# Keeping split MLP weights in DRAM after the first of four token groups

## The chip, the cores and the metric

One core of a Trainium2 chip runs one launch of the kernel. The metric is device time in microseconds (us). TensorE multiplies matrices, VectorE (DVE), ScalarE (ACT) and GpSimd (POOL) work elementwise, and SyncE (SP) issues nearly all DMA transfers between DRAM and the on-chip SBUF. TensorE writes its products to PSUM banks. Each engine, SP's queue of DMA issues included, takes its instructions in a fixed order and waits at a semaphore where an input is not there or a buffer is not free.

## What is computed

The reference is one layer of a streaming encoder over 2064 tokens (16 meta tokens and 2048 frames) of width 1024: RMSNorm, an input projection, an RWKV-7 recurrence for eight heads, forgetting attention for eight heads, then the part that the change touches:

```
h = h + concatenate([y_rw, y_fx]) @ w_o            # 1024 x 1024
h = h + conv_ffn(rmsnorm(h, norm2_g), ...)         # per token group
# conv_ffn: p = x @ w_in (1024 x 5632); causal depthwise convolution of width 3;
#           u, g = split(p); out = (silu(g) * u) @ w_out (2816 x 1024)
```

All data are float32. The kernel multiplies in a float32r type with fewer bits: each operand is split into a rounded high part and the rest as a low part, and a product is made of high x high, high x low and low x high.

## The kernel before

**Stages.** `phase1` makes the projections and the recurrence. `tail` (L1202) then runs attention beside the output projection and the MLP. The MLP works in four groups of some 512 tokens (`FGROUPS`, L1054), each in two blocks of about 256 tokens. Per group `w_o` (L1083) adds the output projection and normalises, and `mlp` (L1188) goes over 22 pieces of 128 channels, two at a time: `up` (L1145) of two pieces, then `down` (L1173) of the two pieces before them. One pass through that loop uses six weight blocks of 128 x 1024: two for each `up`, two for the `down`. A group has eleven such passes. The first group runs beside attention, the second partly; the third and fourth run alone.

**Weights.** Every group loads all weights anew: `weight` (L1070) calls `split_weight` (L74), which issues one DMA of 512 KB on SP into `ww_raw` (L78), lets ACT round it into `ww_hi` (L81) and DVE subtract to get `ww_lo` (L82). The rings are (3, 2) at L1206: three buffers for `ww_hi`, three for `ww_lo`, two for `ww_raw`. A ring's buffer is written again once TensorE has done its last product with it. The first group's `w_o` is cut in two halves of the input channels (`PARTS`), so its blocks are 128 x 512 and there are sixteen.

**Products.** `product` (L1077) issues, for one PSUM bank, first all products with the high weights and high inputs, then high weights with low inputs, then low weights with high inputs. In `up` a bank takes 24 matmuls with one weight block; with two token blocks and two weight blocks that is 96 per call. In `down` a bank takes six matmuls with the two blocks of the pair, and all sixteen banks' worth of them use both blocks.

**Order of the work.** The order on each engine is not that of the program text. The builder (L1292, `schedule_with_timeline_sim=True`) orders the instructions ahead of time by its own estimate of when each could start, earlier program text first among those that are ready, and then fixes one queue per engine. On the chip nothing is reordered.

**DRAM scratch.** `trunk` (L1256) takes scratch tensors from a DRAM pool for operands that pass between stages.

Of the kernel before, what the change touches and what calls it, by code (L numbers as in the profile page):

```python
# [26 lines left out]
# columns of the packed per-feature parameters  # L27
# [8 lines left out]
# columns of the constant input  # L36
# [4 lines left out]
# rings of tiles of RWKV's columns, by tags  # L41
# [3 lines left out]
FXPOS = (10, 11)                           # groups of the recurrence that come before the attention's operands  # L45
class Pool:
    """A tile pool whose tiles get numbered names."""
# [15 lines left out]
def pools(*args):  # L63
    """a function that takes tiles from one of several pools, by their tags; the last one for the others"""
    *ps, where = args
    return lambda shape, tag, bufs=1, dt=F32: ps[where.get(tag, -1)](shape, tag, bufs, dt)
# [7 lines left out]
def split_weight(K, sp, src, shape, tag, bufs, raw_bufs=1):  # L74
    """DMA a weight block and split it into two float32r parts (hi + lo)."""
    nc = K.nc
    raw = sp(shape, tag + "_raw", bufs=raw_bufs)
    nc.sync.dma_start(raw, src)  # L78
    hi = sp(shape, tag + "_hi", bufs=bufs, dt=F32R)
    lo = sp(shape, tag + "_lo", bufs=bufs, dt=F32R)  # L80
    nc.scalar.copy(hi, raw)  # L81
    nc.vector.tensor_sub(lo, raw, hi.bitcast(F32))  # L82
    return hi, lo


def split(eng, K, src, hi, lo):
    """src as a sum of two float32r parts"""
    K.nc.scalar.copy(hi, src)
    eng.tensor_sub(lo, src, hi.bitcast(F32))


def spread(K, pool, r, n, out, root=True):
    """r [tokens, n tiles of g groups] -> r^-1/2 (or r as it is), repeated over the features of its group, [features, tokens]."""
# [12 lines left out]
def phase1(K, ctx, outer, mixer, between):  # L106
    """RMSNorm, input projection, RWKV and attention operands (all [feature, token])."""
    nc, tc = K.nc, K.tc
    # tiles that are needed longer lie higher, for the MLP to take their place early
# [8 lines left out]
    K.idle = sp                            # tiles that the part after the recurrence's operands leaves free  # L118

    # derived parameter columns: 1-mu, w0/2, a0/2, k_a/2, 1-k_a/2, -q_g/8  # L120
# [20 lines left out]
    TT = tp([128, 4, 17, 64], "TT")        # (I - A_ab)^-T of each head and chunk of the half  # L141
# [3 lines left out]
    ahead = None                           # scaled tiles of the next half's first block  # L145

    def norm_scale(t0, n, tags):
        """tiles of 128 tokens of [t0, t0+n), scaled by 1/rms and by g1"""
        o = PC["g1"][0]
        for s in range(0, n, 128):  # L150
# [3 lines left out]
            # the place of the inverses is free  # L154
# [9 lines left out]
            if t0 == 0:  # L164
                # at the start the columns of the last block are free
# [21 lines left out]
    def norm_split(slot, tiles):  # L187
        """hi/lo [128, 8, n] float32r of the scaled tiles"""
# [30 lines left out]
    def head_sums(out, x, hi, lo):  # L219
        """sums of x over the features of a head, on each of them"""  # L220
# [4 lines left out]
    def rw_part(rp, half, blocks, xb):  # L225
        """RWKV columns: token shift, low-rank parts, decays; the operands of the recurrence go to DRAM."""
# [5 lines left out]
        def tmp(ring):  # L232
            """the next tile of a ring, some of them from tags of the attention's part"""
# [5 lines left out]
        def shift(p, M, n, np_, m, out):  # L239
            """token shift: out = (1-mu) h[t] + mu h[t-1]; pads of the last chunk are zero."""  # L240
# [11 lines left out]
        # the last 32 of the gate's inputs three times: [hi; hi; lo] of the weights, [hi; lo; hi] of the inputs  # L252
        gup2 = rp([128, 1088], "k2b", 2, F32R)[0:96, 0:512]
        thad = rp([128, 1088], "thad")
        # --- low-rank inputs: wd|ad, gd (160) and the forget logits
# [56 lines left out]
        # --- RWKV pairs of heads  # L312
        def k_part(p_):
# [5 lines left out]
            for b, (t0, n) in enumerate(blocks):  # L319
# [6 lines left out]
                # normalised kk  # L326
# [14 lines left out]
                # decay  # L341
# [11 lines left out]
                # in-context learning rate: ta = tanh((a0 + ad a_up)/2), a = (1+ta)/2  # L353
# [20 lines left out]
                # A_ab^T (rows s, columns t > s): first head on partitions 64-127, second on 0-63  # L374
# [62 lines left out]
    def invert(rp, parts, nc_, n):  # L437
        """T^T = (I - A_ab)^-T in place in TT: diagonal blocks of n by forward substitution, one system per
        partition (SY[s][t] = A^T, X[j][t] = T^T); then T21 = T2 A21 T1 on the tensor engine."""
# [35 lines left out]
    def merge(rp, pp, T1):  # L475
        """T21 = T2 A21 T1 of the 64x64 inverses (its transpose into TT)"""
# [19 lines left out]
    def gate_part(blocks, xb):  # L496
        """output gate of the attention heads; block by block, so that the normalised columns are free early"""
# [13 lines left out]
    def fx_part(blocks, xb):  # L511
        """attention heads: q, k normalised per head, v transposed"""
# [57 lines left out]
def forget_cumsum(K, sp, sm):  # L570
    """c = cumsum(log_sigmoid(fl + b_f)) along the tokens, for the 8 heads."""
# [11 lines left out]
    nc.vector.tensor_tensor(s, e, d, op=ALU.mult)          # s = e/(2+e); log1p(e) = 2 atanh(s)  # L583
# [7 lines left out]
    # running sums of each piece, then the totals of the pieces before it  # L591
# [15 lines left out]
def layout(inp):  # L607
    """Host side: only lays the inputs out (transposes, reshapes, concatenations, constants of the shapes)."""
# [34 lines left out]
    mu[1824:1856] = mu[1856:1888] = mu[1792:1824]      # as the columns of wg2  # L643
# [16 lines left out]
    # RWKV mask for [k~;b~] rows s against [a~|r~] columns t: s < t for a~, s <= t for r~  # L660
    s, t = i % 64, i % 64
    cst[:, CM : CM + 128] = np.where(i[None] < 64, s[:, None] < t[None], s[:, None] <= t[None])
    # causal mask of a diagonal attention block, added to c: 0 where key <= query
    cst[:, CIN : CIN + 128] = np.where(i[None] <= i[:, None], 0.0, 1e30)
    # pieces before a piece, of the same head
# [23 lines left out]
PA, PB, PCH = 2, 1, 1                      # banks of the products, the solutions and the chain  # L689


def rwkv(K, ctx, part):
    """RWKV-7 recurrence in chunks of 64 tokens; a group is 2 chunks (at the end 1) of all 4 pairs of heads.

    The first head of a pair (h0) has its k~ rows on partitions 0-63 and its b~ rows on 64-127, the
    second (h1) the other way round, so that their small products use different parts of the array.
    What does not depend on the state is worked out ahead of the chain over the chunks, in two steps that
    overlap with it.
    """
    nc, tc = K.nc, K.tc  # L700
    side = "right" if part else None
    # what the last group norm needs lies above, for the attention to take the place of the others early
# [7 lines left out]
    kr = HS                                # rows of k~ and V of each head  # L710
    br = HS[::-1]                          # rows of b~, A~ and U of each head

    # h0 I v a~ r~, h1 r~ a~ v I; the identities stay
# [5 lines left out]
    def products(G):  # L719
        """the products of a group among k~, b~, a~ and r~, and its transposes; slots are chunk-major"""  # L720
# [3 lines left out]
        kb = K.idle([128, KC, 128], ("T1", "sq0")[odd]).rearrange("p a (j e) -> p a j e", e=64)[:, :n]     # h0 k~ b~, h1 b~ k~  # L724
# [4 lines left out]
        # KG: h0 [k~;b~ natural | A_r^T], h1 [A_r^T | b~;k~ natural];  AA: A_ak^T  # L729
        G.KG = KG = sp([128, NS, 2, 128], "KG", 2)  # L730
        AA = sp([128, NS, 64], "AA", 2)
        for c in range(0, n, 4):
            for h in range(2):
                gp = ps([128, 4, 128], "pa", PA)
                rhs = xv[HS[h], :, 2 - 2 * h : 4 - 2 * h]        # h0 a~ r~, h1 r~ a~
# [5 lines left out]
        # natural layouts: KG gets k~, b~; VU: V; AN slot 0: A~  # L741
# [17 lines left out]
    def solve(G):  # L759
        """U0 = T A_ak V, the update of the state M' and R' with T applied to A~"""  # L760
        ch0, ncl, xv, KG, VU, AA, AN = G.ch0, G.ncl, G.xv, G.KG, G.VU, G.AA, G.AN
        n = 4 * ncl
        # AN slot 1: A_ak V
# [5 lines left out]
        # [T A~ | U0] = T [A~ | A_ak V]  # L769
# [9 lines left out]
        # MT: h0 [I + M' | r~ + R'], h1 [r~ + R' | I + M']  # L779
# [8 lines left out]
    def chain(G):  # L788
        """the chain over the chunks; the state's rows 0-63 are h0, 64-127 h1, block diagonal"""
        ch0, ncl, KG, VU, MT = G.ch0, G.ncl, G.KG, G.VU, G.MT  # L790
        end = ("pb", PB) if ch0 == NCH - 1 else ("ch", PCH)   # the other products are done
        Y = sp([128, 4, 2, 64], "Y", 2)                      # rows: tokens of the two chunks; pair; heads
# [23 lines left out]
    def norm(G):  # L816
        """the group norm and the gate"""
# [6 lines left out]
        # group norm over the 64 channels of a head  # L824
# [31 lines left out]
def attention(K, ctx, name, phases, bufs, banks):  # L856
    """Forgetting attention: a function that adds a phase, of phases: lists of blocks of query tiles of 128 (-1: the
    meta tokens); in each phase one head after the other. mask: the causal mask is added on the tensor engine."""
# [16 lines left out]
    def load_head(h, qa, nk_all):  # L875
# [3 lines left out]
        kq = sp([128, NK + NR], "kq", nhead, F32R)           # k_hi twice, q_hi and q_lo  # L879
# [29 lines left out]
    def pieces(qa, nk):  # L909
        """ranges of tokens to load: keys only, then keys and queries"""  # L910
# [7 lines left out]
    def softmaxes(hd, qt):  # L918
        """softmax of the query tiles of a block; their tiles share one where they fit"""
# [6 lines left out]
    def softmax(hd, i, P):  # L926
        """P = exp(S - max) of query tile i (-1: the meta tokens), [queries, keys], and 1/sum (from -S, as q comes negated)."""
# [44 lines left out]
    def value(hd, qt, soft):  # L972
        """O^T of the query tiles qt: sum over the key tiles of [v_hi | v_lo]^T P^T."""
# [5 lines left out]
        per = 2 if N <= 256 else 1             # key tiles at a time  # L979
# [34 lines left out]
        # 1/sum along the columns of O^T  # L1014
# [20 lines left out]
    # the scores of a block come before the values of the one before  # L1035
# [25 lines left out]
class Ffn:  # L1061
    """Output projection, residual, RMSNorm and the gated convolutional MLP, in four groups of tokens."""

    def __init__(self, K, W, rings):
        self.K, self.W, self.rings = K, W, rings
        nc = K.nc
# [189 lines left out]
def trunk(tc, args, out, shapes):  # L1256
    K = SimpleNamespace(nc=tc.nc, tc=tc, outT=out, **args)
    with ExitStack() as c0:
        dr = Pool(tc, c0, "scratch", DRAM)
        for name, shape in SCRATCH.items():  # L1260
            setattr(K, name, dr(list(shape), "d_" + name))
# [35 lines left out]
```

## Time and profile before

| | |
|---|---|
| time, median of 3 runs | 3463.82 us (3456.46 to 3465.52) |
| span of the profiled execution, first to last instruction | 3459.8 us |
| what lies around that span | not recorded; the span lies within the range of the runs |
| matmuls | 28651 |
| DMA moved | 377.32 MB |

The span is cut into stretches in some views. Busy time of an engine is the time in which it had an instruction under way; PE is TensorE's matmuls, PEld its loads of weights into the array. A matmul's record overlaps that of the next, so the pace of TensorE is read from the distance of starts, not from the duration of one. "What ended the idle time" names the instruction whose semaphore came last before an engine went on.

### The profile page before, as it was taken

What the parts mean: (1) busy time and instruction counts of PE and PEld (TensorE: products, weight loads), DVE (VectorE), ACT (ScalarE), POOL (GpSimd) and SP (SyncE); (2) the same over time, 40 slices, a digit from 0 to 9 for tenths busy, and PEclk for the clock granted to TensorE, in tenths of its full rate; (3) what the DMA queues carried; (4) which work ended last, traced back from release to release, by engine and by line L of the source; (5) the groups of instructions that cost most, each with busy time, mean ns of one, the idle gap of its engine ahead of it and who ended that gap; (6) DMA issues with size and microseconds to landing.
All of it is one profiled execution on the core that took longest, in us unless ns stands there. A gap on an engine that the chain in (4) does not pass through costs nothing.

```text
span 3459.8 us, 73945 instructions
## 1 busy us (share of the span) xinstructions
PE 3373.8 (98%) x28651; PEld 3219.1 (93%) x28651; DVE 2361.0 (68%) x5338; ACT 1762.1 (51%) x4230; POOL 994.2 (29%) x1270
## 2 busy tenths in 40 slices
PE   7999999999999999999999999999999999999999
PEld 7889889988988987999999999999999999999999
DVE  5655576575566757877788777877765667656666
ACT  5543444554344467765666666664444444444443
POOL 4441113344111257533233345312114111131111
PEclk9999999999999999999999999999999999999999
DMA  3455343255534264333323352324224222232222
GB/s 113 119 127 161 95 109 95 96 124 141 147 96 104 81 181 141 105 105 109 93 83 94 98 160 87 94 71 137 95 94 154 92 92 96 94 108 94 93 92 92
DMA packets 354088, 377.32 MB, mean 109 GB/s; under 512 B 169240, under 2 KB 284168, under 8 KB 352712
## 3 DMA queue, kind: packets, MB, share of 16 engines
q1 hardware_dynamic: 353544, 372.52, 36.2%
q8 instruction: 226, 3.70, 0.4%
q14 instruction: 126, 1.03, 0.1%
q0 software_dynamic: 192, 0.07, 0.0%
HBM read 302.22 MB, written 70.27 MB: 108 GB/s over the span
## 4 chain that ended last, share of the span: by engine, by line
PE 80%; DMA 7%; DVE 5%; issue 3%; POOL 2%; ACT 2%; SPq 1%; POOLq 0%; ACTq 0%; DVEq 0%
PE pp L1081 32%; PE pr L1081 12%; PE pj L203 5%; PE pj L205 5%; PE pj L204 5%; PE o L1008 4%; PE pt L995 3%; DMA raw<-d_qk 2%; PE pa L737 2%; DMA xv<-d_var 2%; PE s L946 1%; PE s L948 1%; PE pb L774 1%; PE ch L802 1%; PE pb L785 1%
## 5 line engine op out<-in xcount | busy, mean ns | idle before, releaser
L1081 PE MATMUL pp<-xh,ww_hi 128*128 128x256 f32 (+1 forms) x3072 | 467.6, 284 | 11.6 <-ACT zh L1169 3.5
L1081 PE MATMUL pp<-xl,ww_hi 128*128 128x256 f32 (+1 forms) x3072 | 466.1, 285 | 2.3 <-POOL xl L1143 1.8
L81 ACT CAST ww_hi<-ww_raw 128x1024 fp32r<-128x1024 f32 (+1 forms) x304 | 307.9, 1026 | 314.7 <-PE pr L1081 193.1
L1081 PE MATMUL pp<-xh,ww_lo 128*128 128x256 f32 (+1 forms) x3072 | 456.5, 284 | 0.0
L1170 POOL TENSOR_TENSOR zl<-cv,zh 128x256 fp32r<-128x256 f32 (+1 forms) x176 | 174.0, 989 | 940.8 <-ACT pp L1156 430.7
L82 DVE TENSOR_TENSOR ww_lo<-ww_raw,ww_hi 128x1024 fp32r<-128x1024 f32 (+1 forms) x304 | 370.8, 1230 | 87.0 <-ACT ww_hi L81 77.1
L1081 PEld LDWEIGHTS pp<-xh,ww_hi 128*128 128x128 f32 x3072 | 410.1, 189 | 16.8 <-ACT zh L1169 3.6
L1081 PEld LDWEIGHTS pp<-xl,ww_hi 128*128 128x128 f32 x3072 | 410.4, 190 | 5.9 <-POOL xl L1143 3.5
L1081 PEld LDWEIGHTS pp<-xh,ww_lo 128*128 128x128 f32 x3072 | 405.3, 189 | 1.6
L1004 DVE TENSOR_TENSOR pl<-pt,ph 128x512 fp32r<-128x512 f32 (+4 forms) x416 | 220.6, 538 | 80.0 <-ACT ph L1003 77.0
L1003 ACT CAST ph<-pt 128x512 fp32r<-128x512 f32 (+4 forms) x416 | 190.5, 467 | 161.4 <-PE pt L995 112.9
L1183 DVE TENSOR_TENSOR acc<-acc,pr 128x256 f32<-128x256 f32 x480 | 197.8, 420 | 100.8 <-PE pr L1081 99.3
L1160 DVE SCALAR_TENSOR_TENSOR cv<-pp,pc,cv 128x256 f32<-128x256 f32 (+1 forms) x352 | 168.5, 479 | 137.4 <-ACT cv L1159 134.6
L939 DVE CUSTOM_DVE_ANT_0 P<-cb,s 16x16 f32<-16x16 f32 (+8 forms) x360 | 183.0, 519 | 50.6 <-PE s L948 27.1
L995 PE MATMUL pt<-cst,P 128*128 128x128 f32 (+2 forms) x1224 | 201.7, 276 | 3.6 <-ACT P L965 2.0
L1159 ACT ACTIVATE cv<-pp,pc 128x256 f32<-128x256 f32 (+1 forms) x352 | 201.2, 571 | 0.0
L1008 PE MATMUL o<-ph,vs 128*128 128x256 f32 (+3 forms) x640 | 189.4, 303 | 6.8 <-ACT ph L1003 5.1
L1081 PE MATMUL pr<-zh,ww_hi 128*128 128x256 f32 x960 | 193.9, 282 | 0.1
L1081 PE MATMUL pr<-zh,ww_lo 128*128 128x256 f32 x960 | 192.5, 281 | 0.0
L1081 PE MATMUL pr<-zl,ww_hi 128*128 128x256 f32 x960 | 191.4, 280 | 0.0
L1008 PE MATMUL o<-pl,vs 128*128 128x256 f32 (+3 forms) x640 | 174.8, 290 | 2.2 <-DVE pl L1004 1.8
L1161 DVE SCALAR_TENSOR_TENSOR cv<-pp,pc,cv 128x256 f32<-128x256 f32 (+1 forms) x352 | 169.1, 480 | 6.6
(383 smaller groups left out, 8570.4 us busy)
## 6 DMA issues: line engine op xcount, KB each, us to landing
ww_raw<-in_fin_dram SPq DMA_DIRECT2D x176, 512.0 KB, 3.2
ww_raw<-in_fout_dram SPq DMA_DIRECT2D x88, 512.0 KB, 3.9
w_raw<-in_wt_dram SPq DMA_DIRECT2D x60, 512.0 KB, 3.5
xv<-d_var SPq DMA_DIRECT2D x32, 384.0 KB, 5.9
ww_raw<-in_wo_dram SPq DMA_DIRECT2D x24, 512.0 KB, 3.3
raw<-d_qk SPq DMA_DIRECT2D x112, 88.0 KB, 2.6
cb<-d_cd SPq DMA_DIRECT2D x8, 1032.0 KB, 6.8
out_dram<-acc SPq DMA_DIRECT2D x32, 256.0 KB, 2.8
```

The source lines that it names most:

```text
L81: nc.scalar.copy(hi, raw)
L82: nc.vector.tensor_sub(lo, raw, hi.bitcast(F32))
L203: nc.tensor.matmul(p, wh[:, c, :M], xh[:, c, :n], start=c == 0, stop=False)
L939: nc.vector.tensor_tensor_reduce(dst, c, src, 1.0, 3e38, op0=ALU.add, op1=ALU.min, accum_out=mx[:nq, np_ : np_ + 1])
L995: nc.tensor.transpose(pt[:kn, x, c0 : c0 + nq], P[:nq, k0 : k0 + kn], K.ident[:nq, :nq])
L1003: nc.scalar.copy(ph[:kn, xs, c:N], pt[:kn, xs, c:N])
L1004: nc.vector.tensor_sub(pl[:kn, xs, c:N], pt[:kn, xs, c:N], ph[:kn, xs, c:N].bitcast(F32))
L1008: nc.tensor.matmul(o[:, c:N], vs[:kn, jj], pp[:kn, x, c:N], start=jj == 0 and y == 0, stop=jj == nt - 1 and y == 1)
L1081: self.K.nc.tensor.matmul(p, w, x, start=i == 0, stop=i == len(mms) - 1)
L1159: nc.scalar.activation(v, p[:, 2 : nb + 2], AF.Identity, bias=pcol(K, "cb", i), scale=pcol(K, "cw2", i))
L1170: nc.gpsimd.tensor_sub(zl[:, b : b + nb], u, zh[:, b : b + nb].bitcast(F32))
L1183: nc.vector.tensor_tensor(a, a, p, op=ALU.add)
```

## The change

The first use of a weight block goes as before, and afterwards SP issues two more DMAs, which write the two parts to DRAM tensors. A later use of the same block allots the next buffers of the `ww_hi` and `ww_lo` rings and fills each by a DMA of 512 KB from there; no `ww_raw`, no ACT and no DVE instruction is used. Comment lines removed by the diff are left out here; the rings stay (3, 2).

```diff
         self.K, self.W, self.rings = K, W, rings
         nc = K.nc
+        self.done = set()
+        self.split = {name: [K.dram([n, 128, KC * 128], f"{name}_{t}") for t in "hl"]
+                      for name, n in (("wo", KC), ("fin", 2 * FT), ("fout", FT))}
...
-    def weight(self, src, n=KC * 128):
-        return split_weight(self.K, self.W, src, [128, n], "ww", *self.rings)
+    def weight(self, name, i, cc=range(KC)):
+
+        K, nc = self.K, self.K.nc
+        n = 128 * len(cc)
+        cut = lambda t: t[i].rearrange("p c f -> p (c f)")[:, 128 * cc[0] : 128 * cc[0] + n]
+        src = K.__dict__[name]
+        src = cut(src) if name != "fout" else src[i]
+        kept = [self.split[name][x][i, :, 128 * cc[0] : 128 * cc[0] + n] for x in range(2)]
+        if (name, i, cc[0]) in self.done:
+            both = []
+            for t, k in zip(("hi", "lo"), kept):
+                w = self.W([128, n], "ww_" + t, self.rings[0], F32R)
+                nc.sync.dma_start(w.bitcast(F32), k)
+                both.append(w)
+            return both
+        self.done.add((name, i, cc[0]))
+        both = split_weight(K, self.W, src, [128, n], "ww", *self.rings)
+        for w, k in zip(both, kept):
+            nc.sync.dma_start(k, w.bitcast(F32))
+        return both
...
-                wh, wl = self.weight(K.wo[m, :, cc[0] : cc[-1] + 1].rearrange("p c f -> p (c f)"), 128 * len(cc))
+                wh, wl = self.weight("wo", m, cc)
...
-        w = [self.weight(K.fin[i].rearrange("p c f -> p (c f)")) for i in (f, FT + f)]
+        w = [self.weight("fin", i) for i in (f, FT + f)]
...
-        w = [self.weight(K.fout[f]) for f in fs]
+        w = [self.weight("fout", f) for f in fs]
...
         dr = Pool(tc, c0, "scratch", DRAM)
+        K.dram = dr
```

## Rows read from the trace of the kernel before

**Rows 1.** Engines over the span: busy us (share) xinstructions.

```profile
PE 3373.8 (98%) x28651; PEld 3219.1 (93%) x28651; DVE 2361.0 (68%) x5338; ACT 1762.1 (51%) x4230; POOL 994.2 (29%) x1270
```

**Rows 2.** Stretches of the tail: length, busy us of each engine, clock, DMA share, GB/s.

```profile
core 0: us, PE busy (x) PEld busy (x) DVE busy (x) ACT busy (x) POOL busy (x), PEclk, DMA share, GB/s
...
1400.00:1990.00 590.00, 584.34 (x4589) 565.05 (x4588) 469.86 (x1321) 379.10 (x909) 200.66 (x314) 1.00 0.32 99
1990.00:2400.00 410.00, 403.92 (x3211) 391.76 (x3210) 310.98 (x814) 253.03 (x570) 142.33 (x213) 1.00 0.35 111
...
2460.00:3460.00 1000.00, 988.23 (x8276) 985.35 (x8274) 666.16 (x1284) 428.66 (x1057) 176.51 (x174) 1.00 0.29 100
```

**Rows 3.** Chain that ended last, in order of time: start us, us, instructions.

```profile
3232.50 7.11 PE pr L1081 x60
3239.61 21.87 PE pp L1081 x184
...
3266.66 7.11 PE pr L1081 x60
```

**Rows 4.** Waits of PE from 1990 to 3460: us, times, longest us.

```profile
PE pp L1081 <- ACT zh L1169: 3.5, 1, 3.5
PE pp L1081 <- ACT ww_hi L81: 2.3, 2, 1.1
```

**Rows 5.** Costliest groups of the page: the split of the weights.

```profile
L81 ACT CAST ww_hi<-ww_raw 128x1024 fp32r<-128x1024 f32 (+1 forms) x304 | 307.9, 1026 | 314.7 <-PE pr L1081 193.1
...
L82 DVE TENSOR_TENSOR ww_lo<-ww_raw,ww_hi 128x1024 fp32r<-128x1024 f32 (+1 forms) x304 | 370.8, 1230 | 87.0 <-ACT ww_hi L81 77.1
```

**Rows 6.** DMA issues of weights over the span: count, KB each, us to landing.

```profile
ww_raw<-in_fin_dram SPq DMA_DIRECT2D x176, 512.0 KB, 3.2
ww_raw<-in_fout_dram SPq DMA_DIRECT2D x88, 512.0 KB, 3.9
...
ww_raw<-in_wo_dram SPq DMA_DIRECT2D x24, 512.0 KB, 3.3
...
ww_raw<-in_wo_dram SPq DMA_DIRECT2D x16, 256.0 KB, 3.1
```

**Rows 7.** DMA from 3100 to 3450: queue (packets, MB, share of 16 engines); landings of `ww_raw`.

```profile
q1 hardware_dynamic: 8685, 31.29, 25.9%
...
DMA to landing us min/median/max: 3.1/3.2/6.3
```

**Rows 8.** Timeline of one pass, 3204 to 3229: start us, us, engine, instructions.

```profile
3205.06 2.00 ACT L81 CAST ww_hi<-ww_raw 128x1024 fp32r<-128x1024 f32 x2 [6.76 <-PE pr L1081]
...
3207.12 1.11 PE L1081 MATMUL pp<-xh,ww_hi 128*128 128x256 f32 x8
...
3209.03 0.99 PE L1081 MATMUL pp<-xh,ww_hi 128*128 128x256 f32 x7
...
3209.86 1.11 PE L1081 MATMUL pp<-xh,ww_lo 128*128 128x256 f32 x8
...
3223.30 1.11 PE L1081 MATMUL pp<-xh,ww_lo 128*128 128x256 f32 x8
...
3223.50 1.05 ACT L81 CAST ww_hi<-ww_raw 128x1024 fp32r<-128x1024 f32 x1 [1.08 <-PE pp L1081]
...
3227.10 0.40 PE L1081 MATMUL pr<-zh,ww_hi 128*128 128x256 f32 x2
...
3227.57 0.28 PE L1081 MATMUL pr<-zh,ww_lo 128*128 128x256 f32 x1
```

**Rows 9.** DMA issues from 1400 to 1980: a load and a store of one size.

```profile
d_yd<-og SPq DMA_DIRECT2D x3, 256.0 KB, 3.0
...
og<-d_og SPq DMA_DIRECT2D x4, 256.0 KB, 3.8
```

**Rows 10.** Waits of ACT on attention's loads, 1400 to 2300: us, times, longest us.

```profile
ACT kq L890 <- DMA raw<-d_qk: 50.7, 42, 3.9
...
ACT vs L903 <- DMA raw<-d_vn: 10.5, 11, 2.1
```

## The prediction

> **What bounds the kernel now.** I read the engines over the span first [rows 1]: TensorE is busy for 3373.8 of 3459.8 us, DVE for 68% and ACT for 51%. A busy matmul record is no proof of full pace, so next come the stretches of the tail [rows 2]: from 2460 to 3460 TensorE idles for 11.8 us of 1000, and loads of weights into its array fill 985.35. Then the chain that ended last [rows 3]: it is TensorE alone, in a pass that repeats every 3266.66 - 3232.50 = 34.16 us and holds 288 matmuls, so one starts every 118.6 ns. The pace is the same where weights are loaded, 21.87 us / 184 = 118.9 ns, and where they are not, 7.11 / 60 = 118.5 ns. Last I read what TensorE waits for from the second group on [rows 4]: the split on ACT accounts for 2.3 us. A group has 384 matmuls in its `w_o` and 11 x 288 in its passes, 3552. So the last three groups are bound by the count of matmuls, which the change leaves alone.
>
> **What is removed.** Per group there are 74 blocks (8 of w_o, 44 of w_in, 22 of w_out). The loads agree: 176 = 4 x 44, 88 = 4 x 22, 24 = 3 x 8 and 16 halves [rows 6]. Of 304 splits 222 go, that is 222 x 1.03 = 229 us of ACT and 222 x 1.23 = 273 us of DVE [rows 5]. Neither engine is the bound, so this time is worth only what it keeps TensorE waiting. Upper bound: all of its idle time from 1990 on, 6.1 + 11.8 = 17.9 us [rows 2]. Lower bound: nothing. I take 4 us: the 2.3 us of waits on the cast and about half of the wait for `zh`, 3.5 us, which ACT makes in the same queue as the casts [rows 4].
>
> **What is added in the first group.** The 82 splits (16 of them halves) give 164 writes, 74 x 2 x 0.524 = 77.6 MB. At the rate of a stretch with few small packets, 31.29 MB in 25.9% of 350 us or 345 GB/s [rows 7], that is 225 us of all 16 engines within some 740 us of which 0.32 is used [rows 2]: it fits. On SP each write waits for its cast or subtraction, and attention's loads are queued behind it; ACT already waits 42 + 11 times for those, 61.2 us in all [rows 10]. If a fifth of them came a transfer of 512 KB (0.524 MB / 345 GB/s = 1.52 us) later and that reached TensorE, it would be 11 x 1.5 = about 16 us; if ACT's 36% of idle time [rows 2] covers it, nothing; fewer collisions could also move some waits the other way by a us or two. I take 3 us, near the covered end, since TensorE loses only 5.7 of 590 us there although ACT waits that often. The buffer that is written out stays taken until the write has been read out; TensorE uses a block for 5.7 us or more anyway, and a store of 256 KB lands in 3.0 us beside 3.8 us for a load of that size [rows 9], so I put nothing for it. The Trainium skill ("DMA: Bandwidth & Descriptors", Anatomy of one DMA) speaks against this part: completion "can cause a surprisingly long delay especially when the write target is HBM". By that rule the three stores should land later than the loads; they don't here, and the sum stays as it is.
>
> **What takes the place of the split.** Later groups read 1 MB per block instead of 512 KB. The engines can: 6 x 1.05 MB per 34.16 us is 184 GB/s against 345. What counts is how long after a buffer comes free its new content is there. Before, ACT needs 1.05 us and DVE 1.23 more [rows 5], since the raw block lies ready in its own ring. After, the load itself can only start once TensorE lets go, and a load of 512 KB takes 3.1 us at best, 3.2 in the median, to land [rows 7]; the low part of a block, queued 0.95 us behind the high part, lands at 3.2 - 0.95 + 1.52 = 3.8 us after its own issue, if the two share the engines. A price for the pair that only the Trainium skill states: by its fit for one DMA ("DMA: Bandwidth & Descriptors", Anatomy of one DMA: about 2.0 us and then bytes at 436 GB/s) 1 MB would be there after an estimated 4.4 us, and the shortfall below would shrink by 0.3 us a pass.
>
> With three buffers and six blocks a pass, four blocks have 5 to 11 us from release to first use. Two do not [rows 8]:
> - The second block of `down` takes the buffer of the first block of the `up` before. Its high part is free at 3223.5 and used from 3227.2: 3.7 us, enough. Its low part is free at 3224.4, when the last eight products of `up` with it end, and is used at 3227.57: 3.2 us against 3.8, short by 0.6 us.
> - The second block of the first `up` takes a buffer that the `down` holds to its end. It is free at 3205.06 and used from 3207.12: 2.1 us against 3.2, short by 1.1 us. Its low part is used at 3209.86, 4.6 us after; of the four loads issued together, it lands second or third, after 4.7 or 6.2 us, short by 0.1 to 1.6 us. But here other work can go first: the same block shows it, as 7 high products of the other token block stand at 3209.03 ahead of the low ones. The builder orders by estimated readiness, so it can put 24 products, 2.85 us, of the first weight block in between.
>
> So the stall per pass lies between 0 (all of it covered by order) and about 2.0 us (1.1 + 0.6 and 0.3 of the rest, as one delay covers part of the next). I take 0.6: the first case as it stands, the second covered. Passes with nothing else beside them: 22 in the last two groups; in the second, (8276 - 2 x 3552) / 288 = 4 after 2460 [rows 2], and before that those after attention's end, so that I take 8 of its eleven. 30 x 0.6 = 18 us. The three `w_o`, with 5.7 us per block and a single block in use, have room for 4.7.
>
> **Sum.** - 4 + 3 + 18 = + 17 us on the profiled execution's 3459.8 us; that lies 4.0 under the median of the runs, within their range. On the median: 3463.8 + 17 = 3481, about 0.5% slower.
>
> **The rivals.**
> - Hidden (no change). The builder counts a load as long as or longer than it is, and puts ready products before every late block. For it: the pass already shows such reordering without an idle TensorE [rows 8]. Against it: its estimates must hold for four loads at once. Time: - 4 + 3 = about 3463.
> - ACT and DVE were in the way (faster). The point where it decides is the start of an MLP after `w_o` and the second group beside attention, where DVE is busy for 311 of 410 us [rows 2]. Its price is bounded by the 17.9 us; with four fifths of it, 3463.8 - 14 = 3450. Against it: the split is named in only 2.3 us of waits [rows 4].
> - The doubled traffic slows the matmuls. 118.9 against 118.5 ns with and without loads [rows 3] would give 0.4 ns x 8,640 matmuls (30 passes), 3.5 us: it is inside the range.
> - The change not doing what it says: the first group marks halves of w_o as kept and later groups ask for whole blocks by the key of the first half, which is there; both halves are written by then. I give it no chance.
>
> **How the numbers follow.** About 0.3%, 10 us, is what a measurement of this kernel can tell from no change. Stalls in the ring: 0.51, 3474 to 3512 (up to 1.5 us a pass: 45 + 3 - 4 = 44 and some noise). Hidden: 0.38, 3454 to 3474. ACT and DVE in the way: 0.11, under 3454. So faster 0.11, same 0.38, slower 0.51. The range for 8 in 10, leaving out most of the faster case and the worst stalls (2 us a pass, 3523): 3454 to 3510. The slower case's own range is 3474 to 3512.
>
> **What would show it.** Right: the pass in the last two groups longer than 34.16 us by some 0.6, with TensorE or its weight loads idle before a `pr` product with `ww_lo` or the first `pp` product with a new `ww_hi`, ended by a DMA of `ww_hi` or `ww_lo`; ACT at about 44% and DVE at about 60% over the span; 222 loads more, the DMA queue's share at about 53% (36% and 194 MB more at 345 GB/s); the two waits on L81 gone. Wrong: a pass of 34.2 us with the order of `pp` and `pr` products changed (then it is hidden), a stretch from 1400 to 1990 that grew by more than 10 us (then the writes cost it), or starts of matmuls that lie further apart than 119 ns inside a run without waits.

## The result: 3 per cent slower, and where the time went

The changed kernel takes 3570.48 us, the median of 4 runs (3562.92 to 3577.96), against 3464.60 of the kernel before, run beside it: 1.0302 times as long, with a 95% interval of 1.0282 to 1.0322. The profiled execution took 3570.44 us, its span is 3568.6. The forecast was slower by 17 us; it is slower by 106.

The page of the changed kernel, its engines, its DMA queue (packets, MB, share of the 16 engines), the costliest group that waits, and the DMA issues of the kept weights with their median us from issue to landing:

```profile
PE 3404.3 (95%) x28651; PEld 3245.8 (91%) x28651; DVE 2119.9 (59%) x5116; ACT 1550.9 (43%) x4008; POOL 939.9 (26%) x1270
...
q1 hardware_dynamic: 409128, 566.53, 50.6%
...
L1102 PE MATMUL pp<-xh,ww_hi 128*128 128x256 f32 (+1 forms) x3072 | 478.9, 291 | 76.8 <-DMA ww_hi<-fin_h 67.8
...
ww_hi<-fin_h SPq DMA_DIRECT2D x132, 512.0 KB, 4.0
ww_lo<-fin_l SPq DMA_DIRECT2D x132, 512.0 KB, 4.8
...
fin_h<-ww_hi SPq DMA_DIRECT2D x44, 512.0 KB, 3.8
```

Against [rows 1]: the count of matmuls is the same, DVE and ACT have lost 222 instructions each and 241 and 211 us of work, and TensorE's share fell from 98% to 95%. The third line names the cause that the rest of this document takes apart: the first products of an `up` with the high weights stood idle for 67.8 us until a load of `ww_hi` from DRAM ended. Before, all that the weights made TensorE wait from the second group on were two casts, 2.3 us [rows 4].

**Where.** With a fixed number of matmuls, the count done in a stretch says how far the kernel is. Two stretches of the kernel before, cut at the times that matter here:

```profile
core 0: us, PE busy (x) PEld busy (x) DVE busy (x) ACT busy (x) POOL busy (x), PEclk, DMA share, GB/s
...
2000.00:2600.00 600.00, 593.92 (x4816) 582.29 (x4815) 440.41 (x1054) 330.69 (x763) 161.80 (x228) 1.00 0.32 105
2600.00:3440.00 840.00, 832.37 (x6973) 830.20 (x6972) 562.19 (x1079) 369.07 (x912) 157.27 (x156) 1.00 0.29 101
```

The same stretches of the changed kernel with the one ahead of them, and two short ones of the passes for later:

```profile
1400.00:2000.00 600.00, 593.48 (x4667) 573.29 (x4666) 478.36 (x1332) 381.12 (x921) 210.68 (x324) 1.00 0.61 207
2000.00:2600.00 600.00, 579.70 (x4622) 566.77 (x4620) 351.00 (x976) 262.03 (x688) 145.01 (x233) 0.99 0.49 163
2600.00:3440.00 840.00, 788.27 (x6422) 782.02 (x6420) 368.31 (x852) 211.53 (x689) 113.76 (x148) 0.98 0.51 176
3207.50:3211.00 3.50, 3.45 (x18) 3.48 (x19) 0.00 (x0) 0.00 (x0) 0.00 (x0) 0.59 0.86 335
3246.70:3250.00 3.30, 3.24 (x27) 3.27 (x28) 0.00 (x0) 0.00 (x0) 0.00 (x0) 1.00 0.93 374
```

Read the counts behind PE busy. From 1400 to 2000, where most of the writes lie and the engines' share has doubled, the changed kernel starts 4667 matmuls in 600 us, 7.78 per us, as before (4589 in 590 us [rows 2], also 7.78). Then it falls behind, by 194 from 2000 to 2600 and by 551 from 2600 to 3440, where only passes and the `w_o` of two groups run. There 551 matmuls at 832.37 / 6973 = 0.119 us are 65.8 us: 44.1 of them are idle time (840 - 788.27 against 840 - 832.37), and the rest, 21.7, is pace, 122.7 instead of 119.4 ns per matmul, in a stretch whose granted clock fell from 1.00 to 0.98.

The stages show in the tile `acc`, a group's sums: the first load of its input on SP, the first step of the RMSNorm after `w_o`, and the last store (after xcount: ns min/median/max, then start of the first and of the last, us). Before:

```profile
L1141 DVE SCALAR_TENSOR_TENSOR cv<-acc,pc,pp x32: 448/464/482, 1377.1 to 2137.5; 128x256 f32<-128x256 f32 x24, 128x258 f32<-128x258 f32 x8
L1186 SPq DMA_DIRECT2D out_dram<-acc x32: 332/332/1941, 2017.4 to 3456.4; - x32
...
L1106 SPq DMA_DIRECT2D acc<-in_xT_dram x16: 368/378/733, 1246.2 to 2671.2; - x16
```

And after:

```profile
L1162 DVE SCALAR_TENSOR_TENSOR cv<-acc,pc,pp x32: 453/466/480, 1386.2 to 2129.2; 128x256 f32<-128x256 f32 x24, 128x258 f32<-128x258 f32 x8
...
L1207 SPq DMA_DIRECT2D out_dram<-acc x32: 332/337/742, 2008.8 to 3565.3; - x32
...
L1127 SPq DMA_DIRECT2D acc<-in_xT_dram x16: 373/398/1824, 1245.0 to 2702.1; - x16
```

From the first load to the last store, which leaves out what differs between two executions ahead of the MLP, it is 2320.3 us against 2210.2: + 110. The first `w_o`, load to RMSNorm, took 141.2 us against 130.9; that is 10 of the 110.

**One pass.** The chain that ended last, in order of time, through two passes, with the same load at the ends of a longer row of passes in the third group and in the fourth (start us, us, instructions):

```profile
2817.78 3.50 DMA ww_hi<-fin_h
...
3048.24 3.57 DMA ww_hi<-fin_h
...
3197.00 6.78 PE pr L1102 x58
3203.78 3.63 DMA ww_hi<-fin_h
3207.42 0.14 issue
3207.55 21.71 PE pp L1102 x168
...
3232.40 0.77 DVE acc L1204 x2
...
3233.24 2.14 PE pp L1102 x16
...
3236.09 0.24 PE pp L1102 x2
3236.33 6.78 PE pr L1102 x58
3243.12 3.51 DMA ww_hi<-fin_h
...
3280.15 3.54 DMA ww_hi<-fin_h
...
3512.91 3.50 DMA ww_hi<-fin_h
```

Before, this chain was TensorE alone and came round every 34.16 us [rows 3]. Now it passes through this load in each pass, and the two passes last 3243.12 - 3203.78 = 39.34 and 3280.15 - 3243.12 = 37.03 us. The six passes from 2817.78 to 3048.24 and the eight from 3203.78 to 3512.91 last 38.5 us in the mean, 4.4 more than before. Within a run of products at full clock nothing changed: 6.78 / 58 = 117 ns. The load is the second block of the first `up`, which takes a buffer that the `down` holds to its end. The timeline at that place (start us, us, engine, instruction, and in brackets the idle time before it):

```profile
3203.71 0.40 PE L1102 MATMUL pr<-zh,ww_lo 128*128 128x256 f32 x2
3203.78 0.32 SPq L1085 DMA_DIRECT2D ww_hi<-fin_h  x1
...
3203.94 0.88 PE L1102 MATMUL pp<-xh,ww_lo 128*128 128x256 f32 x6
...
3207.55 1.60 PE L1102 MATMUL pp<-xh,ww_hi 128*128 128x256 f32 x8 [2.73 <-DMA ww_hi<-fin_h]
```

SP issues the load as soon as the `down` lets go, and three more behind it within 1.4 us. Between the end of the `down` and the first product with the new block stand only six products, which end at 3204.82; TensorE then waits 2.73 us. The chain shows why there are only six: of the 24 products that the first weight block of the `up` offers, 16 and 2 were placed into the `down`, ahead of its last 58 and six products. Before, 8 were.

**What follows the wait.** In the first of these passes the granted clock is 0.59 in the 3.5 us behind the wait, a mean between TensorE's two levels, 1.2 and 2.4 GHz, and 18 products take the time of 29. Behind the wait from 3243.12, for a load of 3.51 instead of 3.63 us, it is 1.00 and 27 products fit into 3.30 us. The first pass is longer by 5.2 us: the wait (2.7), the slow products (3.5 - 18 x 0.119 = 1.4) and a wait for DVE's additions (0.8), which leaves 0.3. The second is longer by 37.03 - 34.16 = 2.9 us, about the wait alone. The Trainium skill ("TensorE: Matmul & The Clock Gate", HAM oscillation) describes loops in which every piece of work starts at half clock because the wait for its DMA came before; here the clock fell behind some of the waits and not behind others.

TensorE's waits from 1250 to the end (us, times, longest us):

```profile
PE pp L1102 <- DMA ww_hi<-fin_h: 67.8, 32, 2.8
...
PE pr L1102 <- DMA ww_hi<-fout_h: 2.9, 2, 2.6
```

The 32 waits for `ww_hi<-fin_h` are of two kinds. 23 last 2.5 us or more, 60.9 us together: one for each first `up` of a pass that follows a `down` of its own group in the third and in the fourth group, nine in each, and five in the second. The other nine, in other places as well, come to 6.9 us. Behind the 23, the chain's run of up to 168 products took as long as at full clock (20.2 us for 168) nine times, and 1.3 to 2.8 us longer 14 times. What sets the clock's fall in one pass and not in the next stays open.

So the account comes out: 23 passes at 4.4 us are 101 us, the 110 less the 10 of the first `w_o`.

### The profile page after: what moved, and what is told of

Its sections match the earlier page's. It is cut to its first block, busy times and chain, and to the rows that moved or that the text cites. A ratio compares the mean times of both kernels' runs of the same rounds, so it can differ in the third digit from the quotient of the medians.

```text
span 3568.6 us, 73880 instructions
## 1 busy us (share of the span) xinstructions
PE 3404.3 (95%) x28651; PEld 3245.8 (91%) x28651; DVE 2119.9 (59%) x5116; ACT 1550.9 (43%) x4008; POOL 939.9 (26%) x1270
## 2 busy tenths in 40 slices
DMA packets 409670, 571.31 MB, mean 160 GB/s; under 512 B 175416, under 2 KB 290344, under 8 KB 408296
## 3 DMA queue, kind: packets, MB, share of 16 engines
q1 hardware_dynamic: 409128, 566.53, 50.6%
## 4 chain that ended last, share of the span: by engine, by line
PE 74%; DMA 11%; DVE 5%; issue 4%; ACT 2%; SPq 2%; POOL 1%; POOLq 0%; ACTq 0%; DVEq 0%
PE pp L1102 30%; PE pr L1102 11%; PE pj L205 5%; PE pj L203 5%; PE pj L204 5%; PE o L1008 4%; DMA ww_hi<-fin_h 3%; PE pt L995 3%; DMA raw<-d_qk 2%; PE pa L737 2%; PE s L946 1%; PE s L948 1%; DMA xv<-d_var 1%; PE pb L774 1%; PE ch L802 1%
## 5 line engine op out<-in xcount | busy, mean ns | idle before, releaser
L1102 PE MATMUL pp<-xh,ww_hi 128*128 128x256 f32 (+1 forms) x3072 | 478.9, 291 | 76.8 <-DMA ww_hi<-fin_h 67.8
L1102 PEld LDWEIGHTS pp<-xh,ww_hi 128*128 128x128 f32 x3072 | 420.6, 195 | 88.6 <-issue 74.7
L1102 PE MATMUL pp<-xl,ww_hi 128*128 128x256 f32 (+1 forms) x3072 | 476.6, 289 | 0.4
L1102 PEld LDWEIGHTS pp<-xl,ww_hi 128*128 128x128 f32 x3072 | 422.1, 195 | 2.8 <-POOL xl L1164 0.7
L1191 POOL TENSOR_TENSOR zl<-cv,zh 128x256 fp32r<-128x256 f32 (+1 forms) x176 | 135.0, 767 | 1085.2 <-ACT zh L1190 930.4
L1177 ACT COPY pp<-carry 128x2 f32<-128x2 f32 x352 | 57.2, 163 | 613.9 <-PE pp L1102 612.0
L203 PE MATMUL pj<-xah,w_hi 128*128 128x384 f32 x480 | 166.0, 346 | 1.9 <-ACT xah L194 1.9
```

Of the source, the lines that this page charges most:

```text
L203: nc.tensor.matmul(p, wh[:, c, :M], xh[:, c, :n], start=c == 0, stop=False)
L1102: self.K.nc.tensor.matmul(p, w, x, start=i == 0, stop=i == len(mms) - 1)
```

## The experiments

The theory from these rows: the time goes into one late block per pass, because a ring of three that loads its buffers directly can only start a load when TensorE lets go, and too few products stand between. Rivals: the doubled traffic itself; the late low part (the place that the forecast priced); the writes of the first group.

**A fourth buffer.** The ring of raw blocks, hardly used now, gives one of its two:

```diff
-    F = Ffn(K, W, (3, 2))
+    F = Ffn(K, W, (4, 1))
```

> The changed kernel with rings of four buffers for the high and low weights, paid for by one raw buffer instead of two (the first group alone uses it). Theory A (late buffer: TensorE waits in every pass for one block whose buffer the down projection holds to its end): with a fourth buffer that block has over 5 us from release to use instead of 1, the waits on loads of the high weights (67.8 us, 32 times in the changed kernel) go to under 5 us, a pass is 34.2 us again, and the time is 3450 to 3475. Rival B (the doubled DMA traffic makes loads and engines slower as such): loads still take 4.0 and 4.8 us to land, and the time stays over 3530. Rival C (the writes of the first group cost): over 3475 with the excess before 2000 us of the span.

Measured: 3470.01 us, ratio 1.0035 [1.0021, 1.0049]. The chain of the tail:

```profile
2864.58 22.59 PE pp L1102 x190
...
2898.76 22.59 PE pp L1102 x190
```

TensorE alone again, a pass in 2898.76 - 2864.58 = 34.18 us, 22.59 / 190 = 118.9 ns a product, with the same 1 MB per block as the changed kernel, 571.31 MB over the span in both. So the doubled traffic slows no matmul, and one buffer more gives back nearly all of the loss. The Trainium skill ("Perfetto Trace Analysis", Optimization Strategy) reads a gap that repeats on the engine that should be busy as a possible lack of buffers for the next tile; the 32 waits and this run agree with it.

**More products between, with three buffers.** In `up`, the loops over weight blocks and token blocks are exchanged, so that both token blocks use the first weight block before the second is needed:

```diff
-        for b, nb in G.blocks:
-            y = []
-            for (wh, wl), i in zip(w, (f, FT + f)):
+        y = {b: [] for b, nb in G.blocks}
+        for (wh, wl), i in zip(w, (f, FT + f)):
+            for b, nb in G.blocks:
...
-            u, g = y
+        for b, nb in G.blocks:
+            u, g = y[b]
```

> The changed kernel, rings of three, with the loops of the up projection exchanged: both token blocks with the first weight block, then both with the second. The emitted order then has 40 products (4.7 us) between the end of the down projection and the late block, against 6 in the changed kernel. Theory A: a load of 3.6 us is covered, waits on loads of high weights under 10 us, time 3450 to 3480, with traffic and buffers unchanged. Rival B: over 3530, as traffic is the same.

Measured: 3481.81 us, 1.0078 [1.0053, 1.0103], 2 us over the range that I gave for this theory. Its chain in a pass:

```profile
2856.93 21.88 PE pp L1102 x184
...
2891.10 21.87 PE pp L1102 x184
```

A pass takes 34.17 us with the old ring: in the order on TensorE, 40 products (4.8 us) now stand between the end of the `down` and the late block, and TensorE's waits for `ww_hi<-fin_h` come to 1.3 us in three instead of 67.8 in 32. The rings are as in the changed kernel and so are the bytes; only the order differs. This separates the two halves of the mechanism: the load is late only because too little work lies in front of its first use.

The same exchange in the kernel before, as a control: 

> Control: the kernel before with the loops of the up projection exchanged as in the two kernels by weight block. 3455 to 3470 if the exchange is free; if it costs 10 us itself, what is left of the excess of those kernels is the exchange and not the loads.

3461.47 us, 1.0002 [0.9993, 1.0011]: the order by itself is worth nothing.

**Holding the 24 products back.** In the changed kernel, the third and fourth groups force the first 24 products of an `up` behind the `down`:

```diff
+                with K.tc.issue_after(self.hold) if self.hold else ExitStack():
+                    self.product(p[:, 2 : nb + 2], ...
...
+                self.hold = None
...
                 self.down(G, *prev)
+                self.hold = self.last.ins if G.T0 >= 1040 else None
```

> The changed kernel, rings of three and the loops as they were, but in the third and fourth group the builder is told to queue the first 24 products of an up projection behind the last product of the down projection before it, where it had pulled 18 of them into the down projection. Nothing else in work, traffic or buffers changes. Theory A (the stall is the load's 3.6 us from the release of the buffer less the products between): 24 products instead of 6 leave about 0.4 to 0.8 us a pass in place of 2.7, without falls of the clock, so a pass in the last two groups goes from 37.0 to 39.4 us to 34.6 to 35.3, and the time to 3505 to 3530 (the second group keeps its stalls). If the order in the down projection mattered by itself (TensorE waiting for its PSUM banks): a pass over 36 us.

Measured: 3520.13 us, 1.0177 [1.0161, 1.0193]. The chain:

```profile
2812.46 3.53 DMA ww_hi<-fin_h
...
2847.63 3.64 DMA ww_hi<-fin_h
```

The pass is 35.17 us: 1.0 us over the kernel before, where the changed kernel's are 4.4 over it in the mean. Of that, 0.8 is the load, 3.53 us and 0.14 to the next product, less the 24 products, 2.85. So the 24 products that stand ahead of the late block in the program text nearly cover the load but do not do it alone, and the six that the builder left there cost the rest. TensorE's waits for this load fell to 25.9 us in 27 times, 9.5 us in 17 from 2600 to 3440, and the granted clock from 2600 to 3440 is 1.00: where the wait is short the clock does not fall. Why the builder took 18 products forward was not tried apart.

**Two loads of half the size.** Each kept part is loaded in two DMAs of 256 KB:

```diff
-                nc.sync.dma_start(w.bitcast(F32), k)
+                for s in range(0, n, n // 2):
+                    nc.sync.dma_start(w[:, s : s + n // 2].bitcast(F32), k[:, s : s + n // 2])
```

> The changed kernel with every load of a kept part cut into two DMAs of 256 KB. In the emitted order the late block's first half is asked for 8 products after the end of the down projection, and 20 products of the other token block stand before its second half. Theory A (the stall is the time of one load from release to landing, less the products in between): the first half lands some 2.8 us after issue, so about 1.5 us are lost a pass in place of 2.7, and fewer falls of the clock: 3500 to 3540. Rival B (bytes moved decide): as the changed kernel, 3560 to 3580, as the bytes are the same.

Measured: 3533.02 us, 1.0206 [1.0186, 1.0226]. In its chain the load that is waited for is shorter:

```profile
2882.79 2.81 DMA ww_hi<-fin_h
...
2920.10 2.78 DMA ww_hi<-fin_h
```

2.8 instead of 3.5 to 3.6 us, a pass of 37.31 us here against 38.5 in the mean, and the waits came to 50.4 us in 40 times, 1.3 us in the mean, instead of 67.8 in 32. A shorter time to land shortens the wait: it is the time of one load behind a release, with the bytes over the span unchanged. Half the bytes took off some 0.75 us, so by an estimate from these two landings about 1.5 us of a load's 3.55 go with its size and about 2 do not.

**Only the low part from DRAM.** Later groups load the raw block as before, ACT rounds it, and the low part alone comes from DRAM:

```diff
+            raw = self.W([128, n], "ww_raw", self.rings[1])
+            nc.sync.dma_start(raw, src)
+            hi, lo = (self.W([128, n], "ww_" + t, self.rings[0], F32R) for t in ("hi", "lo"))
+            nc.scalar.copy(hi, raw)
+            nc.sync.dma_start(lo.bitcast(F32), kept[1])
+            return hi, lo
```

> The changed kernel, but later groups load the raw block and round it on ACT as before, and only the low part comes from DRAM. Traffic is that of the changed kernel, DVE's 222 subtractions stay gone, ACT's casts are back. Theory A: the high part of the late block is there 1.05 us after its release again, its low part is needed some 3 us later than the high part, so waits shrink to 0 to 1 us a pass: 3455 to 3495. Rival B: over 3530.

Measured: 3488.82 us, 1.0094 [1.0070, 1.0119]. The chain between two passes:

```profile
2905.28 1.06 ACT ww_hi L1085
...
2939.83 1.06 ACT ww_hi L1085
```

The pass is 34.55 us, and what it goes through is one cast of 1.06 us: the high part. The low part, by the same kind of load as in the changed kernel, is not on this stretch of the chain. In other passes the chain goes through one load of `ww_raw` or `ww_lo` of 5.7 to 7.0 us instead, so not every pass lasts 34.55; but all that TensorE's products waited for low parts from DRAM is 0.9 us in two. So of the two late places the forecast priced the harmless one. It also shows what the split did beside splitting: the raw ring fetched the block early, so that release and first use were a cast apart and not a load.

**Traffic alone, a miss.** The kernel before, with each raw block of the later groups loaded twice into the same buffer and then split, and nothing written (the edit is against the changed kernel):

```diff
+            raw = self.W([128, n], "ww_raw", self.rings[1])
+            nc.sync.dma_start(raw, src)
+            nc.sync.dma_start(raw, src)
+            hi, lo = (self.W([128, n], "ww_" + t, self.rings[0], F32R) for t in ("hi", "lo"))
...
-        for w, k in zip(both, kept):
-            nc.sync.dma_start(k, w.bitcast(F32))
```

> The kernel before, whose later groups load each raw block twice into the same raw buffer and then split it; nothing is written to DRAM. The later groups move as many bytes as in the changed kernel, but ahead of the release of the weight buffers. Theory A: traffic as such costs nothing, 3455 to 3475. Rival B: the later groups are longer by 30 us or more, over 3490.

Measured: 3483.28 us, 1.0064 [1.0040, 1.0088], but not by traffic. The second load waits for the first, and the raw ring becomes late itself:

```profile
2942.56 3.66 DMA ww_raw<-in_fin_dram
...
2946.23 4.63 DMA ww_raw<-in_fin_dram
```

Two loads in series, 8.3 us per raw buffer, lie on the chain, a wait that the changed kernel does not have. The run says nothing on traffic; the fourth buffer, with the same bytes and no wait in the passes, does.

**The writes.** The first group writes as in the changed kernel, the later groups load and split as before:

```diff
         if (name, i, cc[0]) in self.done:
-            both = []
...
-            return both
+            return split_weight(K, self.W, src, [128, n], "ww", *self.rings)
```

> The kernel before plus the 164 writes of the first group; later groups split on the chip as before. Theory A, with writes that fit beside attention: within 0.3% of the kernel before, 3455 to 3475. Rival C (writes on SP hold up attention's loads): 3475 to 3490 with the excess between 1250 and 2000 us.

Measured: 3471.81 us against 3459.70 (10 and 18 runs), 1.0039 [1.0024, 1.0054], about 12 us. Its tile `acc`, with the columns of before:

```profile
L1157 DVE SCALAR_TENSOR_TENSOR cv<-acc,pc,pp x32: 449/464/481, 1379.5 to 2119.8; 128x256 f32<-128x256 f32 x24, 128x258 f32<-128x258 f32 x8
L1202 SPq DMA_DIRECT2D out_dram<-acc x32: 332/332/1731, 2001.4 to 3458.2; - x32
...
L1122 SPq DMA_DIRECT2D acc<-in_xT_dram x16: 367/386/591, 1236.4 to 2672.0; - x16
```

This execution reached the tail 10 us earlier than that of the kernel before, so its end alone would mislead. From first load to last store it took 2221.8 us, 11.6 more than before, and the first `w_o` took 143.1, 12.2 more: in this trace the loss is all there. So the next run leaves out the 32 writes of `w_o` and keeps the 132 of the MLP:

```diff
+        if name == "wo":
+            return split_weight(K, self.W, src, [128, n], "ww", *self.rings)
```

> The kernel before plus the first group's writes of the MLP weights alone (132 writes of 512 KB), without the 32 of w_o, which fall into the stretch from 1247 to 1400 where the attention's loads are densest. If the 12 us of all writes come from that stretch: 3458 to 3466. If they come from the writes beside attention in general: 3467 to 3475.

Measured: 3461.92 us against 3462.01 (12 and 21 runs), 1.0002 [0.9987, 1.0017]; in the trace:

```profile
L1159 DVE SCALAR_TENSOR_TENSOR cv<-acc,pc,pp x32: 450/473/484, 1386.5 to 2142.9; 128x256 f32<-128x256 f32 x24, 128x258 f32<-128x258 f32 x8
...
L1124 SPq DMA_DIRECT2D acc<-in_xT_dram x16: 367/378/697, 1250.6 to 2677.6; - x16
```

The first `w_o` takes 135.9 us, between the 130.9 of before and 143.1, and the intervals of the two ratios do not meet. So where the later groups split as before, the writes of `w_o`, 32 of 164, cost about 12 us, and those of the MLP none that can be measured, at most some 6 by the interval. The trace of one execution is a weaker witness: over all kernels here the first `w_o` took 130.4 to 132.5 us without any write (three traces), 135.9 to 139.6 with those of the MLP alone (three) and 136.9 to 145.9 with all (seven). Which of the things beside it the writes push back was not tried apart.

**Both remedies.** The fourth buffer and the order by weight block still left 10 and 22 us, and both kernels write `w_o`. Two more were to leave that out, by the last edit put on the exchanged loops: one with rings of (3, 2), one with (4, 1).

> Up projection by weight block, rings of three, two raw buffers, w_o split on the chip in every group, the MLP weights kept in DRAM. No pass waits for a load, and what cost between 1247 and 1400 us (writes of w_o, a single raw buffer) is gone. Theory A: 3460 to 3472, no faster than the kernel before beyond what can be measured, as TensorE's count and pace are the same. If loads of kept parts cost beyond the waits: over 3475.

> Rings of four and one raw buffer, the up projection by weight block, w_o split on the chip in every group and never written, the rest kept in DRAM. Theory A: no wait for a load in any pass, and without the writes of w_o the first group is as in the kernel before: 3450 to 3468, at best some 5 to 10 us under it, as TensorE then has the same count of matmuls at the same pace and little idle time left. If the writes of the MLP weights cost too: 3468 to 3480.

Measured: 3470.14 us, 1.0025 [1.0014, 1.0037], with three buffers, and 3476.62 us, 1.0043 [1.0030, 1.0056], with four, which is more than the 3468 that I expected at most without a cost of the writes. From 2600 to 3440 they start 6988 and 6993 matmuls, as many as the kernel before or a few more, so nothing is left of the loss in the passes. Part of what remains lies in the first `w_o` again, here of the kernel with three buffers:

```profile
L1164 DVE SCALAR_TENSOR_TENSOR cv<-acc,pc,pp x32: 460/468/483, 1383.3 to 2128.7; 128x256 f32<-128x256 f32 x24, 128x258 f32<-128x258 f32 x8
L1210 SPq DMA_DIRECT2D out_dram<-acc x32: 332/338/577, 2012.6 to 3467.3; - x32
...
L1129 SPq DMA_DIRECT2D acc<-in_xT_dram x16: 383/387/585, 1244.8 to 2680.8; - x16
```

138.5 us there, 7.6 more than before, of 12.3 more in all (2222.5). It writes no `w_o`, and ACT waits for the raw blocks as little as before; these some 10 us stay open. With a single raw buffer ACT does wait there (waits of ACT from 1247 to 1400 in the kernel with four):

```profile
ACT ww_hi L81 <- DMA ww_raw<-in_wo_dram: 14.7, 11, 2.9
```

The kernel before has 3.7 us in two such waits. The raw buffer given up for the split weights is missing where the first group still splits; that this is what the kernel with four loses was not tried apart. With four buffers, leaving out the writes of `w_o` gained nothing over the first experiment (1.0043 against 1.0035), so their 12 us cannot simply be taken off any version. No version beat the kernel before.

## Why the forecast was right in sign and wrong in size

- **What bounds the kernel.** Held. The count of matmuls and their pace inside a run, 117 to 119 ns, are unchanged; every loss is a place where TensorE stands or runs at a lower clock.
- **What is removed** (- 4 us). The splits went as counted, 222 on each engine, and with them 211 us of ACT and 241 of DVE (229 and 273 forecast); ACT is at 43% and DVE at 59% (44 and 60 forecast). Its worth cannot be told from nothing: no run that took the splits away is faster than the kernel before. The run with four buffers starts 7028 matmuls from 2600 to 3440 instead of 6973, and 55 x 0.119 = 6.5 us there would fit a small gain, but it ends later all the same.
- **What is added in the first group** (+ 3, 0 to 16). Mis-sized: about 12 us by the run with writes only, inside the bounds that I gave. I looked for it among attention's loads beside the MLP; it sits in the 130 us of the first `w_o`, whose 32 writes I had counted with the others. That writes take no longer to land than loads held: 3.8 us against 4.0. The forecast's estimate of 4.4 us for a pair of loads, from the fit of the Trainium skill ("DMA: Bandwidth & Descriptors", Anatomy of one DMA), did not hold: the low part, the second of a pair, took 4.8 us from its own issue in the median. The page gives that fit for DMAs issued by GpSimd, and these are issued by SP.
- **What takes the place of the split** (+ 18). **This step failed**, at the sentence that the second late place can be covered by order: "so it can put 24 products, 2.85 us, of the first weight block in between". The sentence before it speaks of the other token block, so these are that block's 24 products, on top of the 2.1 us of work that stood there before [rows 8]: 5.0 us, more than the load. The run by weight block bears out that they would do it, with 40 products between and passes of 34.17 us. What failed is the step from can to does. The builder put none of them there, and it moved 18 of the 24 products that do stand ahead of the late block to a place ahead of the release, so 0.9 us of work stood there instead of 2.1. The load was mis-sized beside this, 3.4 to 3.7 us with four issued within 1.4 us, against 3.2 for the loads of before [rows 7]. The stall is 2.7 us instead of the upper bound of 1.1 that I had for it. Why the builder chose this order stays open.
- **The first late place**, which I priced at 0.6 us a pass, is free: none of TensorE's products is listed as waiting for a low part of a `down`. The high parts of a `down` cost 2.9 us in two waits.
- **How often, and how much.** I took 30 passes at 0.6 us. The long wait came only where an `up` follows a `down` of its own group, which is nine times a group: 23 times in all, at 4.4 us a pass in the mean. So the count was too high and the price too low by a factor of seven. The 4.4 are the wait of 2.65 us, and for the rest the fall of the clock behind some of the waits, waits for DVE's additions and the short waits; this division was read from single passes and not tried apart.
- **The rivals.** Hidden: no. ACT and DVE in the way: not seen. Traffic slowing the matmuls: refuted by 118.9 ns a product with the same bytes. The change does what it says: loads and bytes rose as counted, the queue's share to 50.6% (53 forecast).
- **The range.** It ended at 3510, because the worst stall that I priced was 2.0 us a pass, and even that was left out. It took the order of products of the kernel before as given, with a freedom only to improve; the lower clock after a wait was not in it at all.

## What to carry to other kernels

A stage that copies from a raw ring does two things: it computes, and it makes the refill of the working ring short, a cast of 1.06 us in place of a load of 3.5. Before it is replaced by a direct load, find for every buffer of the ring the work that stands between its release and its next use, and give the ring one more buffer or that work an order in which it is longer than the load. Where a builder orders the products, do not count on ready work to stay behind the release: here 18 of 24 products were used up before it.

## What was unexpected of the hardware

- The granted clock fell to a mean of 0.59 in the 3.5 us behind a wait of 2.7 us, while behind a wait of nearly the same length a pass later it stayed at 1.00. From 2600 to 3440 this is 0.98 in the mean, and at 35.17 us a pass, with waits of about half a us (9.5 us in 17), 1.00 again.
- A load of 512 KB landed in 3.5 to 3.6 us on the chain, and in two halves the same bytes were waited for 2.8 us, without a loss elsewhere that outweighed it: 3533.02 against 3570.48 us.
- 32 writes beside the first `w_o` cost about 12 us in the kernel whose later groups split, where 132 others of the same kind, with the DMA engines at 0.61 from 1400 to 2000 in the changed kernel, cost nothing that twelve runs could tell.
